# Gate tiles in pairs of two by seven products, token sums inside attention, branch maxima read in FFN1

## The chip, the cores and the metric

The kernel is one program on one NeuronCore of a Trainium2 chip. The metric is the device time of one execution in microseconds (us). The engines that matter are TensorE (PE, matmuls and the loading of their weights), VectorE (DVE), ScalarE (ACT), GpSimd (POOL) and SyncE (SP, which issues the DMAs). Each runs its own instructions in order and waits on semaphores for the others. SBUF is the on-chip memory, PSUM the memory into which PE accumulates, in banks of 128 x 512 float32.

## The reference

One decoder layer for 1024 tokens of 1024 features, cut to what the change touches:

```python
x = x + 0.5 * swiglu(rms_norm(x, ffn1_norm), ffn1_w_gate, ffn1_w_up, ffn1_w_down)   # hidden 2816
h = rms_norm(x, mix_norm)
q_lat, kv_lat, k_rope, fq, fk, fv, f_logit, g_mla, g_fox = split(h @ w_in)
y_mla = mla_mixer(q_lat, kv_lat, k_rope, ...)       # 8 heads, causal softmax attention
y_fox = fox_mixer(fq, fk, fv, f_logit, ...)         # 8 heads, cumulative log forget gates
mixed = sigmoid(g_mla + b_gate[0]) * (y_mla @ w_branch_mla) + sigmoid(g_fox + b_gate[1]) * (y_fox @ w_branch_fox)
x = x + mixed @ w_o
x = x + 0.5 * swiglu(rms_norm(x, ffn2_norm), ffn2_w_gate, ffn2_w_up, ffn2_w_down)
```

`g_mla` and `g_fox` are the gates: 1024 columns of `w_in` each. The kernel takes the sigmoid from a tanh.

## The kernel before

Operands are kept as two float16 parts, a high part (ACT's copy with a scale) and a low part (DVE's difference), and a product is three matmuls (high x high, high x low, low x high: lines 156 to 158, helper `mm3`). A matmul has 128 rows of weights and 512 columns of tokens. `split_sb` makes the two parts: line 166 the high one on ACT, line 169 the low one on DVE.

The stages, in order of time: FFN1 (up part, then down part), the normalised and transposed input `h` with its projection, attention, the two branch products, `w_o`, FFN2. In both FFNs and in `w_o` a two by two block of products is done by seven products in place of eight: POOL and DVE form sums of the weight blocks, the tokens' sums are formed once (`token_sums`, around lines 890 to 925), and the results are added after PE. The gates are not done so before.

Attention is a loop of 64 iterations: 8 heads of the MLA kind, then 8 of the FoX kind (iteration 32 on), four query groups each. An iteration issues the scores of two query blocks (`pss`, line 1888), a mask and a maximum on DVE (1890, 1892), exponentials on ACT (1895), transposes on PE (`pspt`, 1914), high and low parts of the transposed probabilities (ACT 166, DVE 169), the product with the values (`pspv`, 1924 and 1929) and its collection into `cmb` (ACT 1931, DVE 1932). This chain alone does not fill PE. Filler is put between: the gates (`gate_steps`, lines 1694 to 1730; 64 steps of 12 matmuls, five of them ahead of the loop, the rest spread over 55 iterations), then the steps of the MLA branch (`branch_mla_steps`, matmuls into `psg`, line 1755 on DVE), whose input pieces start when eight gate steps are left.

A gate step belongs to a half tile: of kind s (MLA or FoX), column tile d (8 of 128) and token half n. The weights of a tile come by DMA and are split once (128x1024 on ACT and on DVE, `whi` and `wlo`); after two steps ACT takes the tanh (line 1725) and SP stores it.

`branch_jobs` (lines 2018 to 2060) loads the two branch matrices in attention, four loads of 1 MB, reads each one's maximum on DVE (line 2031, 128x1024) and works out scales from them in iteration 38.

Other lines that are named below: in the FFNs line 1224 is the down product on PE, 809 a maximum over a weight tile, 866 and 1045 sums on POOL, 898 a token sum's low part, 1129 the addition of a result from PSUM (all but 1224 on DVE or POOL). PSUM has tags for its banks: `psg` and `psb` are those that gates and branches use; a tag with one bank lets the next group of products start only when the last has been read.

What sets the order: the program is written for a framework that keeps, for each engine, a list in the order in which its scheduler emits ready instructions; only some stages are emitted in the order written. Buffers are slots by tag (`u`, `v`, `act`, `wd`, ...) of a few copies each: an instruction that wants a slot waits until its last reader has gone.

```python
while gates and done < total * (i + 1) / 55:
    gates.pop(0)()
    done += 1
if len(gates) <= 8 and pieces:
    pieces.pop(0)()
```

Of the kernel before, what the change touches and what calls it, by code (L numbers as in the profile page):

```python
# [1 line left out]

# [7 lines left out]
F32 = mybir.dt.float32  # L10
# [54 lines left out]
class Layer:  # L65
# [197 lines left out]
    def layer(self):  # L263
# [13 lines left out]
        first = self.start(norm, loads, small, row, tags)  # L277
        mix = self.norm_begin(None, None, ("u", "u"), spill=self.xd, half=True)
# [22 lines left out]
        pending = self.ffn_up(norm, "ffn1", p0, p1, banks, tags, loads, False)  # L301
# [12 lines left out]
        first = self.attention(gates)  # L314
# [144 lines left out]
    def constants(self):  # L459
# [5 lines left out]
        self.ws = c.tile([P, 64], F32, name="ws")  # L465
# [59 lines left out]
    def norm_begin(self, x, g, tags, spill=None, raw=None, sums=None, half=False):  # L525

        st = dict(x=x, g=g, tags=tags, spill=spill, hi=[], lo=[], raw=raw, sums=sums)
        st["dt"], st["s"] = (F16 if half or raw is not None else F32R), None
        return st
# [27 lines left out]
    def norm_parts(self, st, t):  # L557
# [8 lines left out]
        def split():  # L566
            f["h"]()
            f["r"]()
            f["l"]()
# [3 lines left out]
    def norm_steps(self, st, t, engine=None):  # L573
# [40 lines left out]
        late = t in st.get("late", ())  # L614

# [8 lines left out]
        def raw():  # L624
            if t >= 4 and st["raw"] is not None:
                for k in (0, 4):
                    o = st["raw"].rows(k, 4, s)
                    if engine is None:
                        nc.scalar.copy(o, rows(box["ps"], k))
                    else:  # L630
                        engine.tensor_tensor(out=o, in0=h.rows(k, 4, s), in1=l.rows(k, 4, s), op=ALU.add)
# [140 lines left out]
    def up_tiles(self, norm, name, tags, loads, stats, scales, sumd):  # L772
# [4 lines left out]
        def tile(j, ops, tok, finish, mid):  # L777
# [22 lines left out]
            def extra():  # L800
# [3 lines left out]
                if name == "ffn1":  # L804
# [11 lines left out]
                    if k == 4:  # L816
# [5 lines left out]
                        )  # L822
                    for part, at in enumerate((9, 13, 17, 12, 18)):
                        if k == at:
                            self.in_scales(part)
                k = j - 4
# [47 lines left out]
    def token_sums(self, norm):  # L874
# [25 lines left out]
        def total(k, e=None):  # L900
# [8 lines left out]
            elif k == 2:  # L909
                t = src[k, e] = b22  # L910
                v(out=t, in0=t, in1=b12, op=ALU.subtract)
            else:
                t = src[k, e] = b22
                v(out=t, in0=b21[0], in1=t, op=ALU.subtract)
                v(out=t, in0=t, in1=b21[1], op=ALU.add)
# [69 lines left out]
    def in_scales(self, part):  # L985
# [29 lines left out]

        one = self.pow2(wkv, 7, self.ws[:, 39:42])
# [19 lines left out]
    def pair_sums(self, w, stat, norm, scales, j):  # L1036
# [4 lines left out]
        pool = nc.gpsimd.tensor_tensor  # L1041
# [6 lines left out]

        def split(src):
            tag = ("stg", "whi", "wlo", "atp")[self.opn % 4]  # L1050
            self.opn += 1
            o = self.ring.tile([P, 2, 4, P], F16, tag=tag, bufs=2, name="op")
            self.split_sb(o[:, 0], o[:, 1], src, scale)
            return o[:, 0], o[:, 1]

        yield None
        yield split(a11)
        yield split(a12)
        pool(out=a12, in0=a12, in1=s2, op=ALU.subtract)
        self.behind = self.latest(mybir.EngineType.Pool)  # L1060
# [1087 lines left out]
```

## Time and profile before

| | before |
|---|---|
| median of three runs | 2078.96 us (2078.2 to 2080.27) |
| the profiled execution | 2077.2 us |
| its span, first to last instruction | 2075.4 us |
| mean granted TensorE clock | 0.997 |
| busy: PE, DVE, ACT, POOL | 2034.6, 1451.3, 1165.7, 662.1 us |
| first and last scores of attention (line 1888) | 880.5 and 1292.7 us |
| first and last tanh of the gates (line 1725) | 870.6 and 1232.8 us |
| MLA branch steps in attention (line 1755) | 1242.7 to 1302.4 us |

A busy time is the union of the records of an engine's instructions. A matmul's record reaches beyond the start of the next, so the distance between starts tells PE's pace. "Idle before" in a group is the time for which the engine stood still just ahead of its instructions, with the instruction that ended it.

### The profile page before, as it was taken

Reading aid. Unit: us, or ns where it says so; the run is one execution under the profiler, and the core shown is the slowest. Engines: PE = TensorE matmul, PEld = TensorE weight load, DVE = VectorE, ACT = ScalarE, POOL = GpSimd, SP = SyncE. Lnnn points to the kernel's source line nnn. Section 1 sums busy time; section 2 is a strip of 40 time slices with the busy share of each in tenths; the row PEclk is TensorE's granted clock in tenths of the full one; section 3 lists DMA queues with packets and bytes.
Section 4 is the critical chain, followed back from the end, with each engine's and each line's share of the span. In section 5 each row is a group of like instructions: output and inputs, shape, how many; then the busy total and the mean of one; then the engine's idle time right before and its main releaser. Section 6 shows DMA issues by size and latency. Waiting matters only on the chain.

```text
span 2075.4 us, 28646 instructions
## 1 busy us (share of the span) xinstructions
PE 2034.6 (98%) x10247; PEld 1105.9 (53%) x10247; DVE 1451.3 (70%) x2453; ACT 1165.7 (56%) x1961; POOL 662.1 (32%) x727
## 2 busy tenths in 40 slices
PE   8999999999999999999999999999999999999999
PEld 4444444444447555566666666478444444444445
DVE  7856666778887688567767788863765555449876
ACT  6666665545564444466666775421666666555552
POOL 4454544752200112112222222000254555564300
PEclk9999999999999999999999999999999999999999
DMA  8258675465535465656545774541554554355432
GB/s 229 76 148 270 202 241 178 169 231 173 166 125 178 154 173 154 184 144 195 137 122 145 194 194 141 187 148 52 135 144 136 185 181 140 119 197 204 142 112 112
DMA packets 277433, 338.09 MB, mean 163 GB/s; under 512 B 22042, under 2 KB 206218, under 8 KB 277291
## 3 DMA queue, kind: packets, MB, share of 16 engines
q1 hardware_dynamic: 277290, 336.27, 52.7%
q8 instruction: 80, 1.31, 0.3%
q14 instruction: 63, 0.51, 0.1%
HBM read 242.42 MB, written 93.81 MB: 162 GB/s over the span
## 4 chain that ended last, share of the span: by engine, by line
PE 78%; DVE 12%; ACT 4%; DMA 3%; issue 2%; SPq 0%; POOL 0%; ACTq 0%; DVEq 0%; POOLq 0%
PE pst L1071 19%; PE psd L1224 15%; PE psb L1071 11%; PE psg L1071 3%; PE pss L1888 3%; PE pspt L1914 3%; DVE op L169 2%; PE psgate L156 2%; PE psgate L158 2%; PE psgate L157 2%; PE pspv L1924 2%; PE psb L158 2%; PE psb L156 2%; PE psb L157 2%; PE psin L158 1%
## 5 line engine op out<-in xcount | busy, mean ns | idle before, releaser
L1071 PEld LDWEIGHTS <-op 128*128 128x128 f16 x3360 | 328.7, 98 | 389.9 <-DVE s_u L1119 1.8
L1224 PE MATMUL psd<-op 128*128 128x512 f16 x1680 | 364.7, 379 | 2.3 <-DVE op L169 1.4
L1224 PEld LDWEIGHTS <-op 128*128 128x128 f16 x1680 | 164.3, 98 | 201.0 <-issue 4.2
L169 DVE SCALAR_TENSOR_TENSOR op<-s_u,s_v,op 128x512 f16<-128x512 f32 x170 | 149.9, 891 | 90.0 <-ACT op L166 89.5
L1071 PE MATMUL pst<-s_v,op 128*128 128x512 f16 x720 | 165.2, 379 | 1.3 <-DVE s_u L1119 1.3
L1071 PE MATMUL pst<-s_u,op 128*128 128x512 f16 x720 | 165.2, 379 | 1.3 <-DVE s_act L1119 1.3
L166 ACT ACTIVATE op<-s_u,s_v 128x512 f16<-128x512 f32 x170 | 118.0, 715 | 84.4 <-PE psd L1224 72.7
L169 DVE SCALAR_TENSOR_TENSOR op<-s_act,s_wd,op 128x512 f16<-128x512 f32 x130 | 119.9, 934 | 57.0 <-ACT op L166 57.0
L1895 ACT ACTIVATE s_act<-pss,nm 128x128 f32<-128x128 f32 (+7 forms) x128 | 94.6, 739 | 84.0 <-DVE nm L1892 78.2
L1934 POOL COPY atp<-cmb 64x128 f32<-64x128 f32 x64 | 19.5, 305 | 325.5 <-DVE cmb L1932 325.5
L1888 PE MATMUL pss<-s_wd 96*128 96x256 f32 (+5 forms) x480 | 115.2, 364 | 0.0
L1045 POOL TENSOR_TENSOR sums<-s_u 128x512 f32<-128x512 f32 x20 | 25.8, 1292 | 253.2 <-PE psa L612 158.8
L169 DVE SCALAR_TENSOR_TENSOR s_v<-pspt,s_v 128x512 f16<-128x512 f32 (+1 forms) x160 | 95.9, 629 | 9.4 <-ACT s_v L166 8.2
L1914 PE MATMUL pspt<-ident,s_act 128*128 128x128 f32 x576 | 91.5, 279 | 7.2 <-ACT s_act L1895 4.8
L156 PE MATMUL psgate<-s_u,whi 128*128 128x512 f16 x256 | 97.7, 382 | 0.2 <-ACT z L1725 0.2
L157 PE MATMUL psgate<-s_u,whi 128*128 128x512 f16 x256 | 97.1, 379 | 0.0
L158 PE MATMUL psgate<-s_u,wlo 128*128 128x512 f16 x256 | 97.1, 379 | 0.0
L166 ACT ACTIVATE s_v<-pspt 128x512 f16<-128x512 f32 (+1 forms) x160 | 82.6, 552 | 21.8 <-PE pspt L1914 20.0
L1892 DVE TENSOR_REDUCE nm<-pss 128x1 f32<-128x128 f32 (+7 forms) x128 | 93.6, 748 | 1.4
L166 ACT ACTIVATE op<-s_wd 128x512 f16<-128x512 f32 x70 | 50.4, 721 | 77.6 <-PE psd L1224 74.3
L166 ACT ACTIVATE op<-s_act,s_wd 128x512 f16<-128x512 f32 x130 | 88.8, 710 | 7.4 <-PE pst L1071 4.1
L1071 PE MATMUL psb<-s_wd,op 128*128 128x512 f16 x360 | 82.6, 379 | 0.0
(553 smaller groups left out, 4521.6 us busy)
## 6 DMA issues: line engine op xcount, KB each, us to landing
sumd<-s_u SPq DMA_DIRECT2D x20, 1024.0 KB
s_u<-in_w_in_dram SPq DMA_DIRECT2D x19, 1024.0 KB
s_wd<-in_ffn_w_down_dram SPq DMA_DIRECT2D x32, 512.0 KB
sumd<-s_wd SPq DMA_DIRECT2D x13, 1024.0 KB
s_wd<-fd SPq DMA_DIRECT2D x48, 256.0 KB
s_act<-in_ffn_w_down_dram SPq DMA_DIRECT2D x22, 512.0 KB
s_wd<-sumd SPq DMA_DIRECT2D x14, 768.0 KB
s_u<-sumd SPq DMA_DIRECT2D x14, 768.0 KB
```

The costliest lines, as they stand in the source:

```text
L156: mm(out, lhsT=lh, rhs=rh, start=start, stop=False)
L157: mm(out, lhsT=lh, rhs=rl, start=False, stop=False)
L158: mm(out, lhsT=ll, rhs=rh, start=False, stop=stop)
L166: self.nc.scalar.activation(hi, src, AF.Copy, scale=scale)
L169: self.nc.vector.scalar_tensor_tensor(out=lo, in0=src, scalar=scale, in1=hi, op0=ALU.mult, op1=ALU.subtract)
L1071: mm(out, lhsT=a[:, k, :], rhs=b[:, k, :], start=start and k == 0 and i == 0, stop=k == n - 1 and i == 2, skip_group_check=True,)
L1224: nc.tensor.matmul(o, lhsT=u[:, r], rhs=w, start=start and m == 0, stop=k == CK - 1 and m == 2, skip_group_check=True,)
L1888: mm(ps[:, b:e], lhsT=a[:, q], rhs=bb[:, b:e], start=k == 0, stop=k == len(passes) - 1)
L1892: nc.vector.tensor_reduce(out=nm, in_=ps[:, :n], op=ALU.max, axis=AX.X, negate=True)
L1895: nc.scalar.activation(pn[:, :n], ps[:, :n], AF.Exp, bias=nm, accum_out=rs[:, i, j:j + 1])
L1914: nc.tensor.transpose(pt[:, o:o + P], pr[m][:, kt * P:(kt + 1) * P], self.ident)
L1924: mm(po[:, :256], lhsT=v[:, kt, :], rhs=slab[:, s, c, e * 256:(e + 1) * 256], start=kt == 0 and s == 0, stop=False,)
```

## The change

Four things are moved or replaced.

1. **Gates.** The first four tiles of the MLA kind (16 steps) stay as they were. The other twelve are done in six pairs of neighbouring column tiles: a pair's two by two blocks (two column tiles by two halves of the features, on two halves of tokens) go by seven products of 12 matmuls each, from sums of weight blocks made by POOL (three 128x512 sums ahead, one in between), each operand split into high and low part (128x512), with token operands that are sums too. Results are put together in a float32 buffer (`e`): copies on ACT, additions from PSUM on DVE, then the tanh and one store for each tile.
2. **Token sums.** The token operands (`h` block sums t1 to t4, high and low) are made on DVE and ACT in 128x1024 parts, attached to iterations 1 to 8 of attention. `h` is kept also as raw float32 (summed on POOL in FFN1's last part) for that.
3. **Branch maxima.** The four loads and the maxima (now four reductions of 128x2048) are moved to FFN1's up tiles 16 to 19, the scales to its end; `branch_jobs` is gone.
4. **Slots and places.** Forget gates' steps move to iterations 0, 3, 5, 6 (from 2, 6, 8, 10); the MLA branch's input pieces start when three gate steps are left (from eight); the values of two head pairs share one `act` slot.

```diff
-        order = [(s, d, n) for s in range(2) for d in range(KD) for n in range(2)]
-        order = order[:24] + [(1, d, n) for n in range(2) for d in range(4, KD)]
+        order = [(0, d, n) for d in range(4) for n in range(2)]
...
+    def gate_pairs(self, every):
...
+        pairs = [(0, 4), (0, 6), (1, 0), (1, 2), (1, 4), (1, 6)]
...
+        def begin(p):
...
+            w = box["w"] = self.slot("act").rearrange("p (a k n) -> p a k n", a=2, k=KD)
+            for a in range(2):
+                c0 = (C_GM, C_GF)[s] + (d + a) * P
+                nc.sync.dma_start(w[:, a], w_in[:, c0:c0 + P].rearrange("(k p) n -> p k n", p=P))
+
+        def sums(p):
...
+            box["gen"] = self.operands(
+                box.pop("w"), self.wsum[4 * s + d // 2][0], tags, "12 11 - s2 s3 22 21 12"
+            )
+            next(box["gen"])
+            box["ops"] += [next(box["gen"]) for _ in range(2)]
+
+        def step(p, q):
...
+            self.product(ps, box["ops"].pop(0), every((1, 0, 3, 5, 6, 2, 4)[q]), first)
+            if q < 5:
+                box["ops"].append(next(box["gen"]))
...
+                if src is None:
+                    nc.vector.tensor_tensor(out=z, in0=ps, in1=z, op=ALU.add)
+                nc.scalar.activation(
+                    z, z if src is None else src, AF.Tanh, bias=self.bg[:, s, d + a:d + a + 1], scale=inv
+                )
...
+            if q in (0, 2, 3):
+                nc.scalar.copy(e[:, q // 3, (q + 1) // 2 % 2 if q < 3 else 1], ps)
+            elif q == 4:
+                out(1, 0, ps)
+            else:
+                out(*{1: (0, 0), 5: (1, 1), 6: (0, 1)}[q])
+            if q == 4:
+                begin(p + 1)
+            if q == 6:
...
+                sums(p + 1)
...
-        jobs = self.branch_jobs()
         chain = self.forget()
-        for i in (2, 6, 8, 10):
-            jobs.setdefault(i, []).append(lambda: next(chain, None))
+        jobs = {}
+        at = lambda i, f: jobs.setdefault(i, []).append(f)
+        for i in (0, 3, 5, 6):
+            at(i, lambda: next(chain, None))
+        for n, (k, e) in enumerate((k, e) for k in (3, 1, 2, 4) for e in range(2)):
+            for f in (sum_of, high, low):
+                at(n + 1, lambda f=f, k=k, e=e: f(k, e))
+        at(8, lambda: begin(0))
+        at(10, lambda: sums(0))
...
-                if len(gates) <= 8 and pieces:
+                if len(gates) <= 3 and pieces:
                     pieces.pop(0)()
...
+                    if 12 < k <= 16:
+                        last = self.latest(mybir.EngineType.DVE)
+                        self.nc.vector.tensor_reduce(
+                            out=self.spare[:, 1691 + k:1692 + k], in_=box.pop("br"), op=ALU.max, axis=AX.X,
+                            apply_absolute_value=True,
+                        )
...
+                    if 12 <= k < 16:
+                        box["br"] = self.branch_load(k - 12, self.slot(tags["pre"]))
...
+                    if k == 18:
+                        self.branch_scales()
```

The places at which the engines' order changes, with each kernel's own line numbers:

DVE at the end of the input projection, before: the splits of the FoX values (`vtf`), the latents (`mlo`, `lt`) and the first squares of the MLA heads (`s_...<-s_v`) follow each other.

```order
L1608 TENSOR_TENSOR lt<-psb,lt 128x2x128
L1611 TENSOR_TENSOR lt<-psb,lt 64x128
L169 SCALAR_TENSOR_TENSOR vtf<-psin,vtf 128x4x64
L1674 SCALAR_TENSOR_TENSOR mlo<-psmt,cols,mhi 128x512
L1677 SCALAR_TENSOR_TENSOR mlo<-psmt,mhi 128x256
L169 SCALAR_TENSOR_TENSOR vtf<-psin,vtf 128x4x64 x2
L1636 TENSOR_REDUCE s_7412<-s_v 128x8
L1637 TENSOR_REDUCE s_7412<-s_v 128x8
```

The same place now (`t_7944` and `s_u` rows of lines 913 to 926 are token sums):

```order
L1631 TENSOR_TENSOR lt<-psb,lt 128x2x128
L1634 TENSOR_TENSOR lt<-psb,lt 64x128
L170 SCALAR_TENSOR_TENSOR vtf<-psin,vtf 128x4x64
L919 TENSOR_TENSOR t_7944<-s_u 128x1024
L170 SCALAR_TENSOR_TENSOR vtf<-psin,vtf 128x4x64
L1475 SCALAR_TENSOR_TENSOR qks<-psft,cols,qks 128x512
L923 TENSOR_TENSOR s_u<-s_u 128x4x256
L913 TENSOR_TENSOR s_u<-t_7944,s_u 128x4x256
L923 TENSOR_TENSOR s_u<-s_u 128x4x256
L1659 TENSOR_REDUCE s_7255<-s_v 128x8
```

Four token sums stand ahead of the heads' squares, and two more a few rows further on.

DVE in the first iterations of attention now, from the collection of one iteration to that of the next but one (`cmb`), with three token sums and the probabilities' low parts (`s_v`), masks and maxima between:

```order
L2028 TENSOR_TENSOR cmb<-pspv,cmb 64x512
L170 SCALAR_TENSOR_TENSOR s_v<-pspt,s_v 128x512
L919 TENSOR_TENSOR t_8001<-s_u 128x1024
L170 SCALAR_TENSOR_TENSOR s_v<-pspt,s_v 128x384
L1986 TENSOR_TENSOR pss<-pss,maskb 128x128 x2
L1988 TENSOR_REDUCE nm<-pss 128x1
L913 TENSOR_TENSOR s_u<-t_8001,s_u 128x4x256
L1988 TENSOR_REDUCE nm<-pss 128x1
L1527 COPY cc<-psb 128x64
L2028 TENSOR_TENSOR cmb<-pspv,cmb 64x512
L923 TENSOR_TENSOR s_u<-s_u 128x4x256
```

Fourteen such sums are spread over the first eight iterations; before, only the attention rows and a gate's `wlo` stood here.

PE behind the last gate step, before (`pspt` are transposes, `pss` scores, `psg` the MLA branch):

```order
L1929 MATMUL pspv<-s_v,s_act 128x256
L1914 MATMUL pspt<-ident,s_act 128x128
L1888 MATMUL pss<-s_wd 128x512 x2
L1888 MATMUL pss<-s_wd 128x384 x2
L1914 MATMUL pspt<-ident,s_act 128x128 x7
L1888 MATMUL pss<-s_wd 128x512 x4
L156 LDWEIGHTS whi
L156 MATMUL psg<-s_u,whi 128x512
```

And now, two iterations behind the last gate step:

```order
L2025 MATMUL pspv<-s_v,s_act 128x256
L2010 MATMUL pspt<-ident,s_act 128x128 x2
L1984 MATMUL pss<-s_wd 128x256 x2
L2010 MATMUL pspt<-ident,s_act 128x128 x10
L1984 MATMUL pss<-s_wd 128x256 x2
L1984 MATMUL pss<-s_wd 128x384 x2
L2010 MATMUL pspt<-ident,s_act 128x128 x3
L2020 LDWEIGHTS s_act
```

Before, branch matmuls into `psg` follow in the same iteration; now five iterations pass with scores, transposes and value products alone, and eleven branch steps come in the six after them.

More of the change, by code (lines that the diff above doesn't have):

```diff
@@ L276, in layer @@
         self.constants()
-        first = self.start(norm, loads, small, row, tags)
-        mix = self.norm_begin(None, None, ("u", "u"), spill=self.xd, half=True)
+        first, tags1 = self.start(norm, loads, small, row, tags), tags
+        tags = dict(t1="u", t2="v", t3="u", t4="v")
+        mix = self.norm_begin(None, None, ("u", "u"), spill=self.xd, raw="u", sums=tags)
+        mix["adder"] = self.nc.gpsimd
         lat = {}
@@ L313, in layer @@
         self.in_proj(hT, gates, lat["mark"])
-        first = self.attention(gates)
+        first = self.attention(gates, mix)
         ws = []
@@ L523, in gain, with norm_begin @@
         return g
-    def norm_begin(self, x, g, tags, spill=None, raw=None, sums=None, half=False):
+    def norm_begin(self, x, g, tags, spill=None, raw=None, sums=None):
         st = dict(x=x, g=g, tags=tags, spill=spill, hi=[], lo=[], raw=raw, sums=sums)
-        st["dt"], st["s"] = (F16 if half or raw is not None else F32R), None
+        st["dt"], st["s"] = (F16 if raw is not None else F32R), None
         return st
@@ L1013, in in_scales @@
         self.mix_s = ts
+        ss, si = self.ws[:, 64:72], self.ws[:, 72:80]
+        v.tensor_scalar(out=ss, in0=s[:, 4:], scalar1=0.25, scalar2=None, op0=ALU.mult)
+        v.tensor_scalar(out=si, in0=inv[:, 4:], scalar1=4.0, scalar2=None, op0=ALU.mult)
+        self.wsum = [(ss[:, k:k + 1], si[:, k:k + 1]) for k in range(8)]
         one = self.pow2(wkv, 7, self.ws[:, 39:42])
@@ L1040, in pair_sums, with operands @@
         scale, scales[j] = self.pow2(stat[:, 1:2], 14, stat[:, 2:5], norm["inv"])
-        pool = nc.gpsimd.tensor_tensor
+        yield from self.operands(w, scale, None, "11 12 - 21 s2 12 s3 22")
+    def operands(self, w, scale, tags, order):
+        pool = self.nc.gpsimd.tensor_tensor
         (a11, a12), (a21, a22) = ([w[:, a, k:k + 4, :] for k in (0, 4)] for a in range(2))
@@ L1047, in pair_sums @@
         pool(out=s2, in0=a21, in1=a11, op=ALU.subtract)
-        def split(src):
-            tag = ("stg", "whi", "wlo", "atp")[self.opn % 4]
-            self.opn += 1
-            o = self.ring.tile([P, 2, 4, P], F16, tag=tag, bufs=2, name="op")
[L1053 to L1060, printed above, removed]
-        for src in (a21, s2, a12, s3, a22):
-            yield split(src)
+        src = {"11": a11, "12": a12, "21": a21, "22": a22, "s2": s2, "s3": s3}
+        yield None
+        for name in order.split():
+            if name == "-":
+                pool(out=a12, in0=a12, in1=s2, op=ALU.subtract)
+                self.behind = self.latest(mybir.EngineType.Pool)
+                continue
+            if tags is None:
+                tag = ("stg", "whi", "wlo", "atp")[self.opn % 4]
+                self.opn += 1
+            else:
+                tag = next(tags)
+            o = self.ring.tile([P, 2, 4, P], F16, tag=tag, bufs=2, name="op")
+            self.split_sb(o[:, 0], o[:, 1], src[name], scale)
+            yield o[:, 0], o[:, 1]
     def product(self, out, op, tok, start):
@@ L1788, in attention @@
             gates.pop(0)()
+        sum_of, high, low, every = self.token_sums(mix)
+        begin, sums, steps = self.gate_pairs(every)
+        gates += steps
         total = len(gates)
[L1790 removed]
         chain = self.forget()
[L1792 to L1793 removed]
+        jobs = {}
[7 more added lines that the diff above has]
+        at(10, lambda: sums(0))
         for i in range(2 * HEADS * GR):
```

117 lines of the change are left out of this document (65 added, 52 removed).

## The prediction

> **What bounds the kernel now.** I first read the totals and the chain that ended last, and one costly group of matmuls.
>
> ```profile
> PE 2034.6 (98%) x10247; PEld 1105.9 (53%) x10247; DVE 1451.3 (70%) x2453; ACT 1165.7 (56%) x1961; POOL 662.1 (32%) x727
> PE 78%; DVE 12%; ACT 4%; DMA 3%; issue 2%; SPq 0%; POOL 0%; ACTq 0%; DVEq 0%; POOLq 0%
> L1224 PE MATMUL psd<-op 128*128 128x512 f16 x1680 | 364.7, 379 | 2.3 <-DVE op L169 1.4
> ```
>
> TensorE (PE) is the bound. The mean of a matmul is no price, though: 364.7 us over 1680 of them is 0.217 us each, and the record says 379 ns, since one starts before the last is written as ended. In the timeline of the gates the starts are 0.215 to 0.22 us apart:
>
> ```profile
> 1199.95 0.38 PE L158 MATMUL psgate<-s_u,wlo 128*128 128x512 f16 x1
> 1200.17 0.38 PE L156 MATMUL psgate<-s_u,whi 128*128 128x512 f16 x1
> 1200.39 0.38 PE L157 MATMUL psgate<-s_u,whi 128*128 128x512 f16 x1
> ```
>
> Then the busy time by stage (columns: stretch, its length, then busy time of PE, weight loads, DVE, ACT, POOL with their counts, granted clock, DMA share, GB/s), and PE's waits from 890 to 1090 us (two rows) and the four longest from 1090 to 1310:
>
> ```profile
> 340.00:440.00 100.00, 100.00 (x480) 47.71 (x478) 63.82 (x92) 55.07 (x83) 62.13 (x45) 1.00 0.56 190
> 500.00:600.00 100.00, 100.00 (x465) 45.37 (x464) 79.43 (x109) 51.07 (x78) 15.12 (x11) 1.00 0.43 137
> 800.00:850.00 50.00, 49.32 (x256) 27.95 (x255) 34.76 (x100) 20.95 (x62) 11.76 (x36) 1.00 0.49 147
> 890.00:910.00 20.00, 18.88 (x116) 12.71 (x115) 16.16 (x37) 15.84 (x30) 4.75 (x16) 1.00 0.70 185
> 910.00:930.00 20.00, 20.00 (x127) 14.00 (x126) 13.15 (x24) 12.09 (x24) 3.46 (x9) 1.00 0.39 99
> 950.00:1050.00 100.00, 99.10 (x610) 68.09 (x610) 70.84 (x125) 64.22 (x131) 21.92 (x49) 1.00 0.60 169
> 1125.00:1150.00 25.00, 24.38 (x152) 16.22 (x151) 19.30 (x44) 16.38 (x35) 4.64 (x12) 1.00 0.38 91
> 1200.00:1225.00 25.00, 23.14 (x142) 15.12 (x141) 21.25 (x33) 17.96 (x33) 7.23 (x11) 1.00 0.86 231
> 1265.00:1270.00 5.00, 3.21 (x22) 2.06 (x20) 4.50 (x8) 2.35 (x7) 1.28 (x4) 1.00 0.69 245
> 1900.00:2000.00 100.00, 99.80 (x463) 45.18 (x462) 85.18 (x114) 51.40 (x78) 24.53 (x17) 1.00 0.39 129
> PE pspt L1914 <- ACT s_act L1895: 1.5, 4, 0.8
> PE pspt L1914 <- DVE cmb L1932: 1.0, 3, 0.4
> PE pspt L1914 <- ACT s_act L1895: 3.3, 7, 1.0
> PE psg L156 <- DVE s_u L1755: 1.8, 1, 1.8
> PE psb L1995 <- ACT r L1993: 1.5, 2, 0.9
> PE pspv L1924 <- DVE s_v L169: 1.2, 1, 1.2
> ```
>
> The reader is to see that PE's idle share in attention grows with DVE's load: 0 to 1% with DVE at 66 to 71%, 2.5% at 77%, 5.6% at 81%, 7.4% at 85%. In the FFNs a DVE at 79 to 85% costs nothing. So attention is where work for DVE has a price.
>
> **What the change takes from PE.** Gates were 32 halves of 24 matmuls, 768. Now 8 halves stay, 192, and six pairs take 7 products of 12, 504: 72 matmuls of 512 columns fewer. At 0.2155 us that is **-15.5 us**. By the 379 ns of the records it would be 27.3, a saving that PE's cadence cannot give.
>
> **What it costs.** DVE's own part of an attention iteration, from the groups (all 64 iterations, gates' lower halves and branch maxima in the last two rows):
>
> ```profile
> L169 DVE SCALAR_TENSOR_TENSOR s_v<-pspt,s_v 128x512 f16<-128x512 f32 (+1 forms) x160 | 95.9, 629 | 9.4 <-ACT s_v L166 8.2
> L1892 DVE TENSOR_REDUCE nm<-pss 128x1 f32<-128x128 f32 (+7 forms) x128 | 93.6, 748 | 1.4
> L1932 DVE TENSOR_TENSOR cmb<-pspv,cmb 64x512 f32<-64x512 f32 x64 | 44.0, 687 | 52.0 <-ACT cmb L1931 51.3
> L1890 DVE TENSOR_TENSOR pss<-pss,maskb 128x128 f32<-128x128 f32 x128 | 34.8, 289 | 18.6 <-PE pss L1888 12.8 <-ACT s_act L1895 2.9 <-ACT s_v L166 2.5
> L169 DVE SCALAR_TENSOR_TENSOR wlo<-stg,ws,whi 128x1024 f16<-128x1024 f32 x26 | 33.9, 1305 | 19.0 <-ACT whi L166 18.6
> L2031 DVE TENSOR_REDUCE ws<-s_u 128x1 f32<-128x1024 f32 x8 | 9.6, 1203 | 0.1
> ```
>
> The first four make 268.3 us, 4.2 per iteration. Prices of what is added: a 128x1024 sum 1.22 us, an operand's lower half 0.74 alone but 1.77 while POOL runs (446.60 against 447.26), a POOL sum 1.27, a reduction of 2048 columns 2.28:
>
> ```profile
> L898 DVE TENSOR_TENSOR s_wd<-s_v,s_wd x2: 1220/1222/1225, 50.4 to 56.4; 128x1024 f16<-128x1024 f32 x2
> 446.60 0.74 DVE L169 SCALAR_TENSOR_TENSOR op<-s_act,s_wd,op 128x512 f16<-128x512 f32 x1
> 447.26 1.77 DVE L169 SCALAR_TENSOR_TENSOR op<-s_wd,op 128x512 f16<-128x512 f32 x1
> 446.83 1.65 POOL L866 TENSOR_TENSOR s_u<-s_u 128x512 f32<-128x512 f32 x1 [2.06 <-DVE s_u L1129]
> L1045 POOL TENSOR_TENSOR sums<-s_u x20: 1262/1272/1659, 1464.7 to 1808.3; 128x512 f32<-128x512 f32 x20
> 363.56 2.28 DVE L809 TENSOR_REDUCE s_wd<-s_u 128x1 f32<-128x2048 f32 x1
> 369.90 0.75 DVE L1129 SCALAR_TENSOR_TENSOR s_u<-pst,s_wd,s_u 128x512 f32<-128x512 f32 x1 [1.72 <-PE pst L1071]
> ```
>
> *End of the input projection.* The token sums are 20 DVE instructions. In the changed order six of them stand between the splits of the last latent tiles, ahead of small steps for which PE's rope and latent matmuls queue. That is 7.3 us for a DVE at 34.76 of 50, where PE has 0.7 us of idle. Between 0 (it fits in DVE's gaps) and 3 (the chain is late by two or three sums): I take **+2**, since PE has nothing spare to run there.
>
> *First eight iterations.* The other 14 sums are 17.1 us. The scores run over 412 us for 64 iterations,
>
> ```profile
> L1888 PE MATMUL pss<-s_wd x480: 274/376/523, 880.5 to 1292.7; 96*128 96x512 f32 x40, 96*128 96x256 f32 x32, 96*128 96x384 f32 x24, 68*128 68x256 f32 x16
> ```
>
> 6.5 each, so eight are 52. DVE at 13.15 to 16.16 of 20 has 34 to 42 in them and comes to 51 to 59, full; behind each sum stand the maxima and lower halves that PE's transposes and probability-value products wait for. ACT gets 8 casts for DVE's 128x1024 sums to follow; at 12 to 16 of 20 they fit. Between 0.5 (the sums fill gaps only) and 6 (the upper count): **+3.5**, the middle.
>
> *The pairs, iterations 8 to 52.* One step is 12 matmuls, 2.59 us of PE. DVE does one lower half (0.74) and three additions from PSUM in seven steps (0.68 each, as the additions of L1932): 1.03 per step. Before, it was 1.305 in four steps, 0.33, and 0.15 for the maxima of L2031. That is half a microsecond more per iteration, and PE's part is 0.3 shorter, with 53 steps on 55 iterations where there were 59. In the FoX half PE itself needs some 3.4 us (below), 5.9 with its step; DVE comes to 4.7 to 5.2 of it, 80 to 88%, where it had 77%. By the windows this moves idle time from 2.5% to between 4 and 7%, of 21 iterations or 123 us: +1 to +6; in the MLA half, where DVE goes from 71% to about 77, another 0 to 2. **+4**. ACT, at 65%, gains 42 upper halves and 18 copies and loses 16 big splits; it stays under DVE.
>
> *The end of attention.* In the changed PE order no filler stands in the five iterations after the last gate step: the MLA branch's input pieces now start when three steps are left, not eight, and its gate loads wait for slots that the token parts hold until then. Before, branch steps followed the gates at once. PE's own share of a FoX iteration: the groups between 1093 and 1293 us have 96 and 40 trios of filler matmuls,
>
> ```profile
> L157 PE MATMUL psgate<-s_u,whi 128*128 128x512 f16 x96 | 36.4, 379 | 0.0
> L157 PE MATMUL psg<-s_u,whi 128*128 128x512 f16 x40 | 15.2, 379 | 0.0
> 1093.00:1293.00 200.00, 192.42 (x1157) 124.05 (x1156) 159.12 (x282) 134.56 (x269) 48.77 (x101) 1.00 0.62 169
> ```
>
> together 408 x 0.2155 = 87.9; 192.4 less that over 31 iterations is 3.4. An iteration without filler is DVE's: 3.7 (its 4.2 with some 0.07 of overlap between neighbours, 446.60 + 0.74 against 447.26) to 5.2, when the lower halves of the branch's input fall in it too. Five times that difference is 1.5 to 9; the middle is about 6, less 1 for stalls that stood there before: **+5**. The filler that was left out is done two steps to an iteration at the end, all through one PSUM bank (psg), which waits for the product with the gate each time: the wait of 1.8 above stands for one such turn, and there are eleven; most have attention work between them. 0 to 3, **+1**.
>
> *FFN1.* Four reductions of 2.28 us go to up tiles in which DVE idles 1.7 at a time (the row at 369.90): hidden; without that cover it would be at most 9.1. Their 4 MB of loads, moved here from attention, come to a DMA that is 56% busy. At FFN1's end some 14 short scale instructions (0.14 each) join a DVE that then splits operands without a gap. 0 to 2: **+1.2**. *POOL's* eight raw sums in FFN1's tail, the forget chain begun earlier and the weight loads on SP, one buffer for a pair that is loaded two steps ahead: 0 to 1, **+0.5**.
>
> Sum: -15.5 + 2 + 3.5 + 4 + 5 + 1 + 1.2 + 0.5 = +1.7. The profiled execution took 2077.2 us around its span of 2075.4, so 2078.9 by its own measure; the median is 1.8 above it: **2080.7 us**. The ends of the terms add to -12.5 and +16.5.
>
> **The rivals.**
>
> *DVE's work is absorbed, as in the FFNs.* For it: 1900 to 2000 us, PE 99.8 beside DVE 85. Then what stays is 1.5 to 4 at the end of attention, 1 in the first iterations and 1 in the pairs: about -10.5, 2068 us. Against it: attention's own windows, where short chains of scores, maxima and exponentials pass DVE in each iteration.
>
> *DVE and POOL collide (slower).* POOL gets 24 sums for the operands in attention, and the operands' lower halves read SBUF twice, as in the row of 1.77. It decides once DVE in the FoX half passes 95%. Were all 42 lower halves 1 us longer, its 20 or so there would fill the 123 us: idle from 6 to 9% (+5); and sums at 1.9 in the first eight iterations put 10 us on a full DVE, of which I count 6. 2080.7 + 11 = 2092. Against it: 24 sums of 1.27 are 30 us in some 280, so few can meet.
>
> *PE's clock falls in the stretch without filler.* After idle times of 1.90 and 0.74 us the clock was once 0.57 over 4 us:
>
> ```profile
> 684.00:688.00 4.00, 3.26 (x13) 1.58 (x12) 2.45 (x7) 2.40 (x10) 0.00 (x0) 0.57 0.69 219
> ```
>
> Against it stands 1265 to 1270, where PE was busy for 3.21 of 5 us at a clock of 1.00. At 0.57 each of the five iterations would need 6 us on PE: 5 x 1.6 = 8 more, 2089. The Trainium skill, "TensorE: Matmul & The Clock Gate", section "A second HAM failure mode: psum-queue depth-cycling", says that short idles between groups of matmuls can make the clock swing to half; by that rule this rival would hold, and the row at 1265 does not bear it out.
>
> *Pair changes stall.* The next pair's weights go into the one buffer only when the last operand is split, two steps (12 us) before its first product. If DMA and POOL need 1.3 us longer at each of five changes: 2087. DMA is 39 to 60% busy over most of attention, which speaks against it; 1200 to 1225, at 86%, for it.
>
> **How the numbers follow.** Forecast 0.41 (its own range 2075 to 2087), absorbed 0.27, collision 0.22, clock 0.04, pair changes 0.06. A difference of 0.2%, 4.2 us, is about what a measurement of this kernel tells from no change. Faster than 2074.8: nearly all of absorbed and a tail of the forecast, 0.29; slower than 2083.1: collision, clock, pairs and the forecast's upper tail, 0.35; between, 0.36. Range 2067 to 2092, to just beyond the outer cases.
>
> **What would show it.** Right: the gates' group shows 192 and 504 matmuls; DVE over 95% for the first 50 us of attention, with PE waits there of 3 us or more; five iterations near its end with no psg or psgate, at 4.2 to 5 us each; waits for token sums before attention. Wrong: PE at 99% through the first iterations and the FoX half (absorbed); lower halves of 1.7 us by the dozen (collision); granted clock under 1 in attention (clock). Were the stretch without filler no longer than the PE work in it, or the sums hidden in gaps, I am too high by five to nine.

## The result and the profile after

The changed kernel takes 2106.73 us (2103.1 to 2108.31) against 2078.58 beside it: 1.0134 times the time before, 95% interval 1.0116 to 1.0151. That is slower by 28 us, far above the forecast (2080.7) and above its range, 2067 to 2092.

The totals and the chain that ended last, of the changed kernel:

```profile
PE 2040.2 (97%) x10175; PEld 1110.7 (53%) x10175; DVE 1504.6 (71%) x2515; ACT 1192.2 (57%) x2013; POOL 708.4 (34%) x759
PE 76%; DVE 11%; ACT 4%; DMA 3%; issue 3%; POOL 1%; SPq 1%; ACTq 0%; DVEq 0%; POOLq 0%
```

PE has 72 instructions fewer (10247 before), as counted; yet its busy time is 6 us longer. The scores of attention run from 884.2 to 1322.7 us, 438.5 us where they took 412.2. What comes behind the last of them lasts 783.8 us, before 782.7. So 26.3 of the 31.1 us between the two profiled executions lie between the first score and the last; the first comes 3.7 us later (884.2, not 880.5).

```profile
L1984 PE MATMUL pss<-s_wd x480: 274/388/881, 884.2 to 1322.7; 96*128 96x512 f32 x40, 96*128 96x256 f32 x32, 96*128 96x384 f32 x24, 68*128 68x256 f32 x16
L1094 PE MATMUL psgate<-s_u,op x360: 376/379/634, 962.6 to 1247.2; 128*128 128x512 f16 x180
L1094 PE MATMUL psgate<-s_v,op x144: 379/379/650, 977.3 to 1233.0; 128*128 128x512 f16 x144
```

The pairs' 360 and 144 matmuls are the 504 expected. Their longest lasted 634 and 650 ns, not 379: a first sign of the clock. Stretches of attention that answer to those shown of before (same columns), and all of it in the last row:

```profile
915.00:935.00 20.00, 18.57 (x114) 12.19 (x113) 18.51 (x28) 15.93 (x31) 4.34 (x7) 1.00 0.44 114
960.00:1060.00 100.00, 93.03 (x561) 63.58 (x562) 74.50 (x131) 68.49 (x140) 31.16 (x52) 0.98 0.47 119
1140.00:1165.00 25.00, 21.62 (x121) 14.71 (x120) 18.42 (x32) 15.94 (x31) 8.87 (x13) 0.86 0.40 107
1255.00:1280.00 25.00, 18.85 (x98) 14.59 (x98) 17.37 (x32) 14.52 (x31) 3.46 (x9) 0.77 0.83 229
884.00:1330.00 446.00, 409.25 (x2401) 272.74 (x2400) 345.02 (x594) 298.60 (x597) 134.10 (x229) 0.96 0.52 138
```

The reader is to see that PE idles 7 to 25% where DVE is not full: 74.5% from 960 to 1060, 18.42 of 25 (74%) around 1150. By the relation that I had read from before (an idle PE where DVE is loaded) stretches with DVE at 74% should have been at 1 to 2.5%. The waits of PE and of ACT in the same time say what it is:

```profile
PE pspt L2010 <- ACT s_act L1991: 17.5, 17, 3.3
PE pspt L2010 <- DVE cmb L2028: 11.7, 7, 4.0
PE psgate L157 <- ACT z L1747: 2.8, 2, 2.0
ACT op L167 <- POOL sums L1070: 13.1, 5, 4.0
```

PE waits for exponentials (`s_act`), and ACT, which makes them, stands for 13.1 us in five waits before an operand's upper half that needs POOL's sum (and 2.4 in a sixth, on another of POOL's lines). One such pair change, in the timelines of ACT, POOL, DVE and PE:

```profile
1140.50 0.98 ACT L167 ACTIVATE s_v<-pspt 128x512 f16<-128x512 f32 x2
1143.88 0.72 ACT L167 ACTIVATE op<-sums,ws 128x512 f16<-128x512 f32 x1 [2.40 <-POOL sums L1068]
1146.57 0.72 ACT L167 ACTIVATE op<-sums,ws 128x512 f16<-128x512 f32 x1 [1.97 <-POOL sums L1070]
1147.20 0.77 ACT L1991 ACTIVATE s_act<-pss,nm 128x640 f32<-128x640 f32 x1
...
1142.58 1.27 POOL L1068 TENSOR_TENSOR sums<-s_act 128x512 f32<-128x512 f32 x1
1143.93 1.27 POOL L1069 TENSOR_TENSOR s_act<-s_act 128x512 f32<-128x512 f32 x1
1145.28 1.26 POOL L1070 TENSOR_TENSOR sums<-s_act 128x512 f32<-128x512 f32 x1
...
1142.71 1.68 DVE L1988 TENSOR_REDUCE nm<-pss 128x1 f32<-128x640 f32 x2
...
1148.12 0.48 PE L2010 MATMUL pspt<-ident,s_act 128*128 128x128 f32 x1 [3.30 <-ACT s_act L1991]
```

ACT stands still for 2.40 and 1.97 us. The exponential of 1147.20 needs a maximum that DVE had done by 1144.4 at the latest: it stands behind two splits in ACT's queue. POOL's sums are late by POOL's own queue: the second half of the pair's weights had landed at 1136.96, but the sums stand behind a head's collection, which ended at 1142.5. PE then waits 3.30 us for the exponential, and after that its clock is low:

```profile
1145.00:1150.00 5.00, 1.88 (x6) 1.59 (x7) 1.76 (x2) 3.43 (x7) 2.72 (x3) 0.69 0.00 0
1150.00:1155.00 5.00, 5.00 (x21) 3.46 (x20) 3.94 (x6) 2.19 (x5) 1.16 (x3) 0.63 0.28 108
```

The books close to within 1 us. PE's waits from the first score to the last add to 35.0 us (9.3 before). The clock was below 1 in twelve stretches of 5 us, which together lack 17.0 us at full speed (0.96 in the row of 884 to 1330 above; none before). 25.7 more in waits and 17.0 of clock, less the 15.5 saved, are 27.2; the scores took 26.3 longer. The 17.0 us come from seven drops of the clock: one at the start of attention (3.4 us lost), three behind pair changes (6.8) and three behind the last gate product (6.8), where PE has no filler for 33.4 us, from the 1247.2 above to the first branch product:

```profile
1280.63 0.38 PE L157 MATMUL psg<-s_u,whi 128*128 128x512 f16 x1
```

### The profile page after: what moved, and what is told of

It is laid out like the page before. It is cut to its first block, busy times and chain, and to the rows that moved or that the text cites. A ratio compares the mean times of both kernels' runs of the same rounds, so it can differ in the third digit from the quotient of the medians.

```text
span 2106.5 us, 28666 instructions
## 1 busy us (share of the span) xinstructions
PE 2040.2 (97%) x10175; PEld 1110.7 (53%) x10175; DVE 1504.6 (71%) x2515; ACT 1192.2 (57%) x2013; POOL 708.4 (34%) x759
## 4 chain that ended last, share of the span: by engine, by line
PE 76%; DVE 11%; ACT 4%; DMA 3%; issue 3%; POOL 1%; SPq 1%; ACTq 0%; DVEq 0%; POOLq 0%
PE pst L1094 19%; PE psd L1247 15%; PE psb L1094 11%; PE psgate L1094 3%; PE psg L1094 3%; PE pspt L2010 3%; PE pss L1984 3%; DVE op L170 2%; PE pspv L2020 2%; PE psb L159 2%; PE psb L157 2%; PE psb L158 2%; PE psin L159 1%; PE psin L157 1%; PE psin L158 1%
## 5 line engine op out<-in xcount | busy, mean ns | idle before, releaser
L1094 PEld LDWEIGHTS <-op 128*128 128x128 f16 x3864 | 374.4, 98 | 439.9 <-issue 6.7
L1247 PEld LDWEIGHTS <-op 128*128 128x128 f16 x1680 | 164.3, 98 | 200.6 <-issue 3.5
L2010 PE MATMUL pspt<-ident,s_act 128*128 128x128 f32 x576 | 97.2, 290 | 30.7 <-ACT s_act L1991 17.5
L1984 PE MATMUL pss<-s_wd 96*128 96x256 f32 (+5 forms) x480 | 123.7, 381 | 0.7 <-DMA s_wd<-mk 0.6
L2030 POOL COPY atp<-cmb 64x128 f32<-64x128 f32 x64 | 24.3, 379 | 290.0 <-DVE cmb L2028 290.0
L2010 PEld LDWEIGHTS pspt<-ident,s_act 128*128 128x128 f32 x576 | 69.3, 147 | 61.3 <-ACT s_act L1991 34.1
L1094 PE MATMUL psgate<-s_u,op 128*128 128x512 f16 x360 | 87.8, 382 | 0.0
L1984 PEld LDWEIGHTS pss<-s_wd 96*128 96x128 f32 (+1 forms) x480 | 82.5, 201 | 8.9 <-ACT s_act L1991 0.9
```

The costliest lines, as they stand in the source:

```text
L1094: mm(out, lhsT=a[:, k, :], rhs=b[:, k, :], start=start and k == 0 and i == 0, stop=k == n - 1 and i == 2, skip_group_check=True,)
L1247: nc.tensor.matmul(o, lhsT=u[:, r], rhs=w, start=start and m == 0, stop=k == CK - 1 and m == 2, skip_group_check=True,)
L1984: mm(ps[:, b:e], lhsT=a[:, q], rhs=bb[:, b:e], start=k == 0, stop=k == len(passes) - 1)
L2010: nc.tensor.transpose(pt[:, o:o + P], pr[m][:, kt * P:(kt + 1) * P], self.ident)
```

## The experiments

Theory A after the result: an operand's upper half that waits for POOL blocks ACT's queue, and idle PE and low clock follow from that. Theory B: the load of the pairs on DVE and ACT is too much for attention's short chains, wherever it stands. "1.0056 (1.0039 to 1.0074)" below is the ratio to the kernel before, run beside it, with its 95% interval.

### e1 and e5: take POOL's sums away; only change ACT's order

```diff
-            box["gen"] = self.operands(box.pop("w"), ...)
+            box["gen"] = self.raw_operands(box.pop("w"), ...)   # e1: splits read raw weight blocks
```

> The changed kernel without POOL's 24 sums of weight blocks for the gate pairs: each operand is split from a raw weight block instead (so the gates' values are not the reference's). All splits, products, additions and loads stay, in number and size. Theory A (ScalarE's queue): at each of the pair starts an operand's upper half waits in ScalarE's queue for POOL's sums (13 to 15 us in all in the changed kernel's trace), the exponentials stand behind it, PE runs dry and its clock falls behind that. Without the sums these waits go, and most of the low clock: 2080 to 2090 us, no wait of ScalarE's split for POOL left. Theory B (load): the pairs' splits and additions are simply too much for VectorE and ScalarE in attention's short chains, and the waits show up wherever the chain is tightest: only the collisions with POOL go, 2101 to 2105 us.

```diff
+                last = self.latest(mybir.EngineType.Activation)
                 self.nc.scalar.activation(o[:, 0], src[name], AF.Copy, scale=scale)
+                self.follow(last)                                # e5: behind the last exponential
```

> The changed kernel, with one more order on ScalarE: the upper half of a gate pair's operand follows the last exponential that was issued before it. No work is added or left out; POOL's sums stay where they are. Theory A (the exponentials stand behind a split that waits for POOL): the exponentials go first, PE's waits for them at the pair changes and the low clock behind them go for the most part, though not as far as without POOL's sums (2089): 2090 to 2098 us. Theory B (the wait moves with the load): the copies and splits behind the waiting one are late instead, 2103 to 2110 us.

e1: 2088.98 us, 1.0056 (1.0039 to 1.0074). e5: 2087.97 us, 1.0050 (1.0034 to 1.0066), a little better than the range I had given. e5 does all the work of the changed kernel and all its sums; the edit adds only an order on ACT, and 18.8 of the 28 us are gone. The lists of the other engines shift with that order, though: the next pair's weights are loaded later (for the pair above at 1135.92 and 1136.36, not 1121.57 and 1128.08), and PE's stretch without filler behind the gates is 12.7 us long, not 33.4. PE's longest waits in e5, then ACT's:

```profile
PE pspv L2028 <- DVE s_v L170: 6.7, 6, 4.1
PE pspt L2018 <- ACT s_act L1999: 5.5, 11, 1.8
PE psgate L157 <- ACT z L1755: 2.7, 2, 1.9
ACT s_act L1999 <- DVE nm L1996: 55.7, 43, 4.0
ACT cmb L2035 <- PE pspv L2033: 26.6, 21, 5.4
```

Waits for exponentials fell from 17.5 to 5.5 us, those for `cmb` from 11.7 to 1.3, and no wait of ACT for POOL's sums is left. The clock's loss fell with them, from 17.0 to 8.5 us. e1, whose gates get other values since its splits read raw blocks, takes 17.8 us away. There these waits of PE fell less, and the clock's loss in attention fell to 3.4 us:

```profile
PE pspt L2022 <- ACT s_act L2003: 12.4, 14, 2.6
PE pspt L2022 <- DVE cmb L2040: 6.1, 5, 2.4
```

Where the time goes, in us of each profiled execution, with the collections of iterations 8, 52 and 63 (`cmb` on DVE) as marks:

| stretch | before | changed | e1 | e5 |
|---|---|---|---|---|
| up to the first score | 880.5 | 884.2 | 885.2 | 884.3 |
| to iteration 8 | 63.7 | 68.6 | 67.4 | 66.4 |
| iterations 8 to 52, the pairs | 284.7 | 295.8 | 277.7 | 287.3 |
| iterations 52 to 63 | 75.0 | 85.3 | 83.5 | 78.3 |
| behind it | 771.5 | 772.6 | 770.8 | 769.7 |

From iteration 8 to 52 the changed kernel has 53 filler matmuls fewer than before, 11.4 us at 0.2155, and yet takes 11.1 us more: 22.5 are lost. By the same count (55 and 51 matmuls fewer) 4.9 are lost in e1 and 13.6 in e5. So, by one execution each, POOL's sums make up 17.6 of the 22.5, and 8.9 go when exponentials stand ahead of splits, with the sums still made; most of the rest of e5's gain, 7.0, is at the end, where its filler lies otherwise. Collisions of POOL with DVE are a small part of the 17.6: the 42 lower halves take 40.8 us in all in the changed kernel and 37.6 in e1. Theory A holds for the pairs. How the other 8.7 us of the sums' price come about is not shown (that the splits themselves are late for PE is a guess), and B is not dead, since some 9.5 us stay in both runs.

### e2: POOL's sums one step earlier

```diff
+            if q == 3:
+                begin(p + 1)
+            if q == 5:
+                sums(p + 1)          # POOL only; the first two splits stay at q == 6
```

> The changed kernel with POOL's three sums of a pair one gate step (about an iteration of 6 us) ahead of the first splits, and to make room the second step yields two operands and the next pair's weights are loaded one step earlier. Nothing else moves in number. Theory A: the upper halves find their sums done; the 13 to 15 us of ScalarE waits and the clock loss behind them go for the most part: 2084 to 2096 us. Theory B: within 3 us of the changed kernel's 2106.7.

2104.33 us, 1.0122 (1.0102 to 1.0142): a miss for the number, at B's end, and not clear of noise from the changed kernel. ACT still waited 8.5 us for POOL:

```profile
1127.80 0.39 SPq L1768 DMA_DIRECT2D s_act<-in_w_in_dram  x1
1142.29 1.27 POOL L1068 TENSOR_TENSOR sums<-s_act 128x512 f32<-128x512 f32 x1
1143.59 0.72 ACT L167 ACTIVATE op<-sums,ws 128x512 f16<-128x512 f32 x1 [2.41 <-POOL sums L1068]
```

The second half of that pair's weights was issued on SP at 1127.80, 6.7 us after the first (1121.09), behind a head's operands; POOL's sums stood in its queue behind another iteration's head collection, and ran at 1142.29. Emitting work earlier did not make it run earlier here, where two queues in order lie between; e5 leaves the sums late and lets the exponentials go first.

### e3, e15, e17: what the token sums cost

```diff
-            for f in (sum_of, high, low):
-                at(n + 1, lambda f=f, k=k, e=e: f(k, e))       # e3; e15 the same in e9's kernel
...
+        order = [(0, d, n) for d in range(KD) for n in range(2)]
-        pairs = [(0, 4), (0, 6), (1, 0), (1, 2), (1, 4), (1, 6)]
+        pairs = [(1, 0), (1, 2), (1, 4), (1, 6)]               # e17, in e9's kernel
...
-                at(n + 1, ...)
+                at(2 * n + 8, ...)
```

> The changed kernel without the token sums: the gate pairs' products read plain token blocks (the gates' values are not the reference's), so 20 VectorE instructions and 8 casts are left out, six of them from the end of the input projection and the rest from attention's first eight iterations. By my prediction's terms (2 + 3.5, and 5.5 by the two traces' iteration times): 2099 to 2102 us. Rival: the sums fit into gaps: 2105 to 2108 us.

> The version with the split behind the exponential and the gates over 60 iterations (2082.2 us), without the token sums (the gate pairs read plain token blocks, so the gates' values are not the reference's). Theory: where nothing else stalls, the sums still cost what two of my terms say, 5.5 us, and the run without them shows what the pairs themselves bring: 2074 to 2077 us. Rival: with room in ScalarE's and VectorE's queues they are nearly hidden: 2079 to 2082 us.

> The version with the split behind the exponential and the gates over 60 iterations (2082.2 us), with eight gate tiles done directly instead of four and four pairs instead of six, so that the token sums have twice the iterations (8 to 22). 24 matmuls of the saving are given back, 5.2 us. The sums cost that version 10.8 us (2071.4 without them). Theory: their price is that of crowding; spread they cost at most 4: 2077 to 2080 us. Rival: they cost the same wherever they stand: 2086 to 2089 us.

In e3 and e15 the pairs' products read plain token blocks, so the gates get other values. e3: 2099.76 us, 1.0104 (1.0083 to 1.0126), 7.0 less than the changed kernel. e15: 2071.38 us, 0.9969 (0.9956 to 0.9982), 10.8 less than e9, more than I expected; it may be that with other stalls in the way part of the price is hidden behind them. e17: 2078.14 us, 1.0006 (0.9997 to 1.0015). It gives back 5.2 us of PE's saving, so 2071.4 + 5.2 = 2076.6 would be free sums, and it lies 1.5 above that, inside its noise. But it also has two pairs fewer, with their splits and additions. If six pairs cost some 11 us beside PE's saving, as e15 has it (below), two are worth 3.7, an estimate, and the spread sums cost about 5, half of 10.8. That would fit a price that comes from crowding, but no run changes the spreading alone.

### e4, e14, e18: all gates direct

```diff
+        order = [(s, d, n) for s in range(2) for d in range(KD) for n in range(2)]   # e4: no pairs, no sums
...
-                if len(gates) <= 3 and pieces:
+                if len(gates) <= 8 and pieces:                 # e14
...
-        for i in (0, 3, 5, 6):
+        for i in (2, 6, 8, 10):                                # e18: forget chain as before
```

> The changed kernel with all sixteen gate tiles done directly as before (768 matmuls) and without token sums and pairs; the branch maxima in FFN1, the raw sums in FFN1's tail, the moved forget chain, the shared slots and the threshold of three steps stay. Theory: pairs and token sums cost it, so this comes back to 2079 to 2086 us (the later start of the MLA branch is still in it, up to 5 us). Rival: the slots, the late branch start or FFN1 cost it, then it stays at 2095 us or more.

> The run with all gates done directly (2083.5 us), and the MLA branch's input pieces begun when eight gate steps are left, as before, instead of three. That run had lost 7 us between iteration 52 and 63 against the kernel before. Theory: the threshold is what makes the branch late, these come back: 2076 to 2079 us. Rival: the slots that the raw sums and the shared pieces hold make its gate loads late: 2082 to 2085 us.

> All gates direct, branch pieces begun when eight gate steps are left (2075.8 us), and the forget chain back in iterations 2, 6, 8 and 10 as in the kernel before. What is left of the change is the branch maxima in FFN1, the raw sums in FFN1's tail and the shared value slot. Theory: the moved chain costs the start of attention 3 to 5 us (tables loaded ahead of the first scores): 2070 to 2073 us, faster than the kernel before by more than the noise. Rival: the chain costs the same there: 2075 to 2078 us.

e4: 2083.48, 1.0025 (1.0012 to 1.0038). e14: 2075.79, 0.9987 (0.9978 to 0.9997). e18: 2075.74, 0.9987 (0.9978 to 0.9996). Three things follow. Pairs and sums together cost 23.2 us (2106.7 - 2083.5), the saving of PE's 15.5 already taken off. The late start of the MLA branch's input costs 7.7 (e4 to e14). And what else is left of the change (the branch maxima out of attention, the raw sums, the shared slot) gains 2.7 on the kernel before; I take it for the maxima, but no run moves them alone. The forget chain's move is worth nothing either way. Scores of e4 and of e14:

```profile
L1979 PE MATMUL pss<-s_wd x480: 277/387/587, 882.3 to 1299.9; 96*128 96x512 f32 x40, 96*128 96x256 f32 x32, 96*128 96x384 f32 x24, 68*128 68x256 f32 x16
L1979 PE MATMUL pss<-s_wd x480: 277/369/523, 882.1 to 1291.6; 96*128 96x512 f32 x40, 96*128 96x256 f32 x32, 96*128 96x384 f32 x24, 68*128 68x256 f32 x16
```

They start alike and end 8.3 us apart. With the pairs the pieces would, as I read the slots, gain nothing from starting at eight: they would wait for the slot of the last pair's weights, whose splits come later. That was not tried.

### e7, e12: fill the end of attention

```diff
-                while gates and done < total * (i + 1) / 55:
+                while gates and done < total * (i + 1) / 60:   # and the branch from iteration 61
```

> The changed kernel with the gate steps spread over 60 iterations instead of 55; the MLA branch's steps start in iteration 61 and all but five are done behind the loop. The stretch without filler (85 us from iteration 52 to 63 against 75 before) should go: theory, it costs 8 to 12 us and these come back: 2095 to 2100 us. Rival: PE's work lacks elsewhere or VectorE, not the filler, sets the end: 2104 to 2108 us.

> The kernel before with its gate steps spread over 60 iterations instead of 55 and the MLA branch from 61 on. Its branch steps follow the gates without a gap, so there is nothing to fill: within 3 us of 2078.5. Rival: PE's idle time at attention's end (some 8 us from 1235 on in its trace) shrinks too: 2071 to 2075 us; then the spreading is worth the same with and without the change.

e7: 2095.70, 1.0082 (1.0064 to 1.0100): 11.0 us come back. e12, the same in the kernel before: 2079.85, 1.0011 (0.9999 to 1.0023), no gain: there the filler had no gap. So the stretch without filler is the change's own, and cost about twice what I had put for it (5 and 1).

### e6, e11, e13, e16: the forget chain beside the token sums

```diff
-        for i in (0, 3, 5, 6):
+        for i in (2, 3, 5, 6):     # e6; e11 with totals on POOL; (2, 5, 6, 7) in e13 and e16
```

> The changed kernel with the first part of the forget chain in iteration 2, as before, instead of iteration 0 (the other parts stay in 3, 5 and 6). In the changed kernel its logarithm brings two loads of activation tables of 1.28 us each into the time ahead of the first scores, a gate's tanh waits for them, PE for its bank (1.98 us), and the clock is at half for 3 to 7 us behind that. Theory: the start of attention comes 3 to 5 us earlier, 2101 to 2104 us. Rival: the table loads cost the same two iterations later, 2106 to 2108 us.

> As the run before it, with the forget chain's first part in iteration 2. On a VectorE with room the later chain should cost as little as in the kernel before: 2 to 4 us less than that run. Rival: 0 to 4 us more, as it was beside the token sums on VectorE.

> The version with the split behind the exponential, gates over 60 iterations and the token totals on POOL (2080.1 us), with the forget chain's parts in iterations 2, 5, 6 and 7 instead of 0, 3, 5 and 6. In the two runs with 2, 3, 5, 6 PE waited up to 4 us in its queue for the chain's own second part, which stood one iteration behind the first. Theory: with three iterations between them that wait is gone and the start of attention is as early as with the chain in iteration 2: 2075 to 2078 us. Rival: the chain's small VectorE and ScalarE steps cost the same anywhere beside the token sums: 2080 us or more.

> As the first run of this call, with the gates over 57 iterations, so that eight branch steps find room in the loop and fewer are left behind it. PE's work is the same; if the end of attention is PE's in either case, within 2 us of that run. Rival: a stretch without filler appears again: 2 to 6 us more.

2110.19 (1.0156), 2090.27 (1.0067), 2085.12 (1.0035) and 2092.32 us (1.0065; 1.0050 to 1.0080): the first three slower than the same kernels with the chain at 0, by 3.5 (the intervals overlap), 10.2 and 5.0, and e16 by 7.2 more than e13. I was wrong four times here. What PE waited for first in e11 from 860 to 960:

```profile
PE psb L1536 <- DVE s_act L1526: 4.0, 1, 4.0
PE psb L1537 <- POOL s_act L1530: 3.4, 1, 3.4
```

These are the chain's own matmuls, in PE's queue before DVE and POOL have made their input. In e13, with three iterations between, 2.6 of it was left. Without token sums the chain's place costs nothing (e14, e18), so it is its place beside them that costs; which engine is short there is not shown. In e16 the longest stretch without filler is 19.2 us, in e13 14.7, which fits its rival; but its clock also lost 3.4 us more at the start of attention, so the 7.2 are not the stretch's alone.

### e8, e9, e10: mended versions

> The three edits of the other runs of this call together (split behind the exponential, forget chain's first part in iteration 2, gates over 60 iterations). If the causes are apart and their prices add, 2106.7 less 8 to 16, less 3 to 5, less 8 to 12: 2074 to 2088 us. If they share one cause (the low clock, or one full engine), no less than 2095 us.

> The changed kernel with two edits: the split behind the exponential, and the gates over 60 iterations; the forget chain stays in iteration 0. Together with the chain's move these gave 2087.8, and that run had lost some 6 us more than the changed kernel up to iteration 8. Theory: the chain's move was a loss of about 5 us and the other two edits add: 2080 to 2085 us. Rival: they share the low clock and do not add: 2087 to 2090 us.

> As the run before it in this call, and the token sums' twelve totals are made by POOL instead of VectorE (2.4 us each instead of 1.2), their casts and lower halves one iteration later, the casts behind the last exponential. If the first eight iterations are set by a full VectorE, they lose 3 to 6 us of their excess of about 6 and the end of the input projection 2: 2074 to 2080 us. Rival: POOL's sums slow VectorE's splits that read SBUF twice, or the collection of the heads on POOL comes late: 2083 to 2090 us.

e8 (e5, e6 and e7 together): 2087.81, 1.0047 (1.0031 to 1.0063); e6 was a loss in it, for e9 (e5 and e7 alone) takes 2082.16, 1.0016 (1.0005 to 1.0027). e10 (e9, and POOL makes the twelve totals, with their casts behind the last exponential):

```diff
+            v = self.nc.gpsimd.tensor_tensor      # in total(), for the gates' sums
...
-                at(n + 1, ...)
+                at(n + (1 if f is sum_of else 2), ...)
```

2080.09, 1.0009 (1.0000 to 1.0018), 2.1 us less than e9, which just misses the 2074 to 2080 that I expected if a full DVE set the first eight iterations. They take 66.2 us in e10 and 66.6 in e9; what came earlier, by 2.3 us, is the first score. Mended, the change comes to where it started, no further. e14 and e18, 0.13% below the kernel before, have no pairs.

## Why the prediction was wrong

Each by its step:

- **-15.5 us of PE work: right.** 72 matmuls fewer. But in e15, with ACT's order mended, the end filled and no sums, only 4.4 us of it arrive (2071.4 against e14's 2075.8). So pairs that compute with no token sums still cost about 11 there, where I had +4; the two kernels also differ in how the filler is spread, for which e12 shows no gain.
- **End of the input projection, +2: right.** Its last products start at 867.1 us, not 865.2, having begun at 689.4, not 689.7: 2.2. Without token sums (e3) the stretch is as short as before, 690.3 to 865.7.
- **First eight iterations, +3.5: the place right, the size too small, the mechanism not shown.** With the term before it 5.5; measured 7.0 (e3) and 10.8 (e15). But DVE was not over 95% for the first 50 us: it was busy for 40.66 of the 50 from 884 to 934, and above 90% only from 915 on (18.51 of 20). And e10, which takes twelve sums off DVE, leaves these iterations as long as they were. What sets them stays open.
- **The pairs, +4: the step that failed.** I priced ACT's part by its load ("it stays under DVE") and not by what its queue waits for. The upper halves wait for POOL's sums, and behind them stand the exponentials. In the pairs' iterations 22.5 us are lost, not 4; without POOL's sums 4.9 (e1), close to my price for the load, and with the exponentials put first 13.6 (e5). I had the place as a rival (the pair changes stall, 0.06), but with DMA as its cause and 1.3 us for each change; it is POOL's queue, in which sums and head collections stand in a row, and ACT waits 1.6 to 4.4 us for it in five of the six pairs.
- **End of attention, +5 and +1: place right, size half.** 11.0 by e7, 7.7 by e14 for the threshold alone. The stretch without filler is 33.4 us long, where I had put five iterations of 4.2 to 5.
- **FFN1, POOL, forget chain, +1.7: too high.** The input projection begins at 689.4, before at 689.7, and the forget chain's move is worth nothing (e14, e18). These two runs are 2.7 and 2.3 below the kernel before; e14's iterations 8 to 52 take 280.8 us, not 284.7, which is where the maxima stood.
- **The clock rival (0.04): it came, not in place of the others but on top.** The row of 1265 to 1270 before, 1.8 us idle at full clock, was one case and I took it for a rule. Here single waits of 1.2 to 4.0 us, alone or two or three together, lost 17 us of clock, 6.8 of them in the stretch without filler, where I had put 8. The Trainium skill's section that I cited ("TensorE: Matmul & The Clock Gate", "A second HAM failure mode: psum-queue depth-cycling") said that short idles do this; the trace agrees (after 1.98 us of idle, 0.57 from 890 to 895).
- **Absorbed, collision:** neither. DVE is at 74% where PE idles, so it is not absorbed and not full, and of the 42 lower halves five took more than 1.5 us.

The sum as the runs give it: 2078.5, less 2.7 (e14), plus 7.7 for the late branch (e4), plus 23.2 for pairs and sums. By the table, the 31.1 us between the two executions are 3.7 ahead of the first score, 4.9, 11.1 and 10.3 in attention and 1.1 behind it. The prices do not add exactly: e5 and e7 together gain 24.6 where the two alone make 29.8, since both shorten the end of attention.

## What to carry to other kernels

An instruction's price on a busy engine is its duration; on an engine that runs in order it is also the wait for its input, paid by all that stands behind it. So for every added instruction ask who makes its input and how late that may be, on each of the engines between, and put it behind the urgent work of its queue. Filler that ends early leaves PE to the short chains: 11.0 us here. And where a scheduler makes the lists, an edit of one order moves others: read an experiment's gain stage by stage before calling it the price of one cause.

## What the hardware showed

The granted clock of PE fell after waits of 1.2 to 4.0 us, and each time for a nearly fixed time. After 1.98 us of idle at 888 the gates' matmuls started 0.43 us apart, twice the 0.2155, up to 894:

```profile
887.99 0.59 PE L157 MATMUL psgate<-s_u,whi 128*128 128x512 f16 x1 [1.98 <-ACT z L1747]
892.13 0.63 PE L157 MATMUL psgate<-s_u,whi 128*128 128x512 f16 x1
892.56 0.63 PE L158 MATMUL psgate<-s_u,whi 128*128 128x512 f16 x1
892.98 0.63 PE L159 MATMUL psgate<-s_u,wlo 128*128 128x512 f16 x1
```

Each drop lost 1.7 or 3.4 us of full speed (at 1145 to 1155, 0.69 and 0.63 over 5 us each: 1.55 + 1.85 us). At half clock that is about 3.4 or 6.8 us long; the trace's record of the granted clock has four drops of 3.4 us and three of 6.8 in attention. In the 3.4 us ahead of each, PE idled for 1.6 to 2.8 us in all; in the kernel before, 1.7 us within 3.4 (the row of 1265 to 1270) brought none, so these traces give no sharp limit. A wait of PE therefore cost more than its length here: 25.7 us more of waits came with 17.0 of clock.
